# The order of wide and narrow matmuls in the products of an up projection

## The chip, the cores and the metric

The kernel runs on one core of a Trainium2 chip. The metric is device time in microseconds; a kernel's time is the median of its runs. The engines are named as in the profile: PE is the matrix engine (TensorE) and PEld its weight loads, DVE is VectorE, ACT is ScalarE, POOL is GpSimd, SP is SyncE, which issues the loads from HBM.

## The reference

One encoder layer on 512 positions with 2048 channels, all in float32. A first part (normalisation, input projection, convolution group and neighbourhood attention, output projection) ends in a residual x. The part that matters here is the gated MLP behind it:

```python
xn = rms_norm(x, ffn_norm_g[l])
up = jnp.einsum("bsd,df->bsf", xn, w_up[l])          # 2048 -> 2 x 5632
up = depthwise_conv(up, ffn_dw_w[l], ffn_dw_b[l])    # width 3 along the sequence
gate, val = jnp.split(up, 2, axis=-1)
x = x + jnp.einsum("bsf,fd->bsd", jax.nn.silu(gate) * val, w_down[l])
```

A last RMSNorm follows.

## The kernel before

Activations lie transposed: 128 channels on the partitions, 512 positions along the free axis. A float32 product is done with three products of parts: every operand is split into a high part (rounded to the matmul's format, `fp32r`) and a low part (what is left), and high x high, high x low and low x high are added up in PSUM. For weights, `parts` (L111) does the split for a tile of 8 blocks of 128 x 128: ACT writes `whi` (L114), DVE writes `wlo` (L115).

The up projection works on f = 0 to 43, each with 128 gate columns and 128 value columns. For each f the two output tiles (gate and value) by two halves of the sequence form a 2 x 2 block product, and the kernel does it with seven products instead of eight (a scheme of Strassen's kind): `factors` (L585) makes the seven combinations of weights, with DVE additions at L596 to L607, and `comb[c][k]` (tiles `xc`) holds the seven combinations of the activations, computed once. A product has eight steps k over the contraction, 8 x 128 = 1024 channels.

A tile `comb[c][k]` is 128 x 512: the high part of 256 positions in the left half, the low part in the right half. So in `up` (L638), function `product`, one matmul of 512 columns with `whi` (L648, called wide) gives high x high in the left half of a PSUM tile and high x low in the right half, and one matmul of 256 columns with `wlo` (L649, called low) adds low x high into the right half. Each matmul has its own weight load (PEld). For k = 0 the wide comes first and clears the accumulator; for k = 7 the wide comes last and closes it. In between they take turns, wide and low. Behind the last wide, `tick` (L657) lets one step of other staged work be issued and `between` (L658) may put in a stretch of the down projection. The two halves of the PSUM tile are then taken by ACT (L662, tiles `vv` and `pl`) and DVE.

The first four f go through `up_apart` (L705) instead, with three matmuls of 256 columns per step and nothing staged between. The other 40 f go through `up`: 40 x 7 = 280 products.

The down projection runs between the products, on the hidden values of the four f before: `down` (L757), two units of weights for most f, one behind product 3 and one behind product 6, each two output tiles of 4 steps with three 512-column matmuls (L125 to L127), whose result ACT copies (L768) and POOL adds into a DRAM tensor by DMA (L769).

The order of weight units is a list, `plan`, made beforehand; `weights` (L146) keeps three units ahead (`AHEAD`), with four buffers each for `whi` and `wlo` and seven for the raw tiles that SP loads. Within an engine, the program order is that of the code, apart from priorities that the first part uses.

Of the kernel before, what the change touches and what calls it, by code (L numbers as in the profile page):

```python
# [16 lines left out]
P = 128  # L17
# [17 lines left out]
U = 8  # L35
# [5 lines left out]
H = S // 2  # L41
# [25 lines left out]
def layer(ctx: ExitStack, tc: tile.TileContext, xT, w_in, w_out, w_up, w_down, par, tab, out):  # L67
    nc = tc.nc
# [16 lines left out]
    def t2(name, dt=F32):  # L85
        return tp.tile([P, S], dt, tag="t2k", name=name)
# [45 lines left out]
    def tick(behind):  # L132
        for todo in (steps, asteps):
            while todo:
                try:
                    with tc.issue_after(behind.ins):
                        next(todo[0])
                    break
                except StopIteration:
                    todo.pop(0)  # L140
# [5 lines left out]
    def weights():  # L146
        at = weights.at
        weights.at += 1
        while len(made) < min(at + 1 + AHEAD, len(plan)):
            made.append(plan[len(made)]())  # L150
        return made[at]
# [75 lines left out]
    ps = psa.tile([P, S], F32, tag="po", name="idle")  # L227
# [17 lines left out]
    for step in ORDER:  # L245
        i = next(a_ if step == "a" else q_)
# [283 lines left out]
    comb = [[] for _ in range(7)]  # L530
# [107 lines left out]
    def up(f, between):  # L638

        def product(c):  # L640

            w = weights()
            ps = (psa.tile([P, S], F32, tag="po", name="pu") if c == 6 else
                  psm.tile([P, S], F32, tag="mm", name="pu"))
            for k in range(U):
                hi, lo = (w[i][:, k * P:(k + 1) * P] for i in range(2))
                m = comb[c][k]
                wide = lambda: nc.tensor.matmul(ps, hi, m, start=k == 0, stop=k == U - 1)  # L648
                low = lambda: nc.tensor.matmul(ps[:, H:], lo, m[:, :H], start=False, stop=False)  # L649

                if k < U - 1:
                    wide()
                    i = low()
                else:
                    low()
                    i = wide()
            tick(i)  # L657
            between(c)  # L658
            return ps[:, :H], ps[:, H:]

        def copy(to, ps):
            nc.scalar.activation(to, ps, AF.Copy)  # L662

        def pair(name):
            return t2(name).rearrange("p (i t) -> p i t", i=2)

        def both(x):
            return x.unsqueeze(1).broadcast_to([P, 2, H])


        vv, low = pair("vv"), pair("pl")
        for i in range(2):
            m, l = product(i)
            copy(vv[:, i], m)
            copy(low[:, i], l)
        m7, l = product(2)
        add(vv, vv, low)
        low = pair("pl")
        copy(low[:, 0], l)
        m1, l = product(3)  # L680
        copy(low[:, 1], l)
        uu, v = pair("uu"), pair("vl")
        u, u2 = uu[:, 0], uu[:, 1]
        add(u2, m7, low[:, 0])
        add(v, vv, both(u2))
        m6, l = product(4)
        add(u, m1, low[:, 1])
        low = pair("pl")
        copy(low[:, 0], l)
        add(u2, u, m6)  # L690
        m2, l = product(5)
        add(u2, u2, low[:, 0])
        add(v, v, both(u2))
        add(vv[:, 1], vv[:, 1], u2)
        low, g = pair("pl"), pair("g")
        copy(low[:, 0], l)
        add(g[:, 0], u, m2)
        m3, l = product(6)
        copy(low[:, 1], l)
        add(g[:, 1], vv[:, 1], m3)  # L700
        add(g, g, low)
        g, v = (t.rearrange("p i t -> p (i t)") for t in (g, v))
        return g, v
# [218 lines left out]
```

## Time and profile before

| | |
|---|---|
| median of 3 runs | 2068.48 us (2067.77 to 2069.17) |
| span of the profiled execution | 2066.8 us |
| PE busy | 2046.6 us, 99% |
| DVE busy | 1664.6 us, 81% |
| ACT busy | 1065.4 us, 52% |
| granted PE clock, mean | 0.997 |
| HBM | 132 GB/s over the span |

The span runs from the first to the last instruction of one execution; the runs' times include what lies around it. Busy time of PE counts a matmul from its start to its modelled end, and matmuls overlap; so two matmuls that follow each other closely both count their whole length only where the view lists them one by one, while the busy time of the engine counts the time covered. A group's row on the page shows how many instructions it has, their busy time added up, the mean duration of one, and the idle time before them. The timeline lists single instructions by start time.

### The profile page before, as it was taken

The numbers are of one execution on the slowest core, as the hardware profiler recorded it, in microseconds if no ns is written. First come the engines' busy times: TensorE is split into PE (matmuls) and PEld (weight loads), VectorE is DVE, ScalarE is ACT, GpSimd is POOL, SyncE is SP. The second block draws the span as 40 slices with busy tenths as digits, with TensorE's granted clock in tenths as the row PEclk, the third lists the DMA queues.
The fourth block names the chain that finished last, engine by engine and source line by source line (L and its number), as shares of the span: only waits on it lengthen the run. The fifth ranks groups of instructions, "written<-read, shape, count | busy, mean of one in ns | idle before, by whom it ended". The sixth has DMA issues, their size and how long they took to land.

```text
span 2066.8 us, 28555 instructions
## 1 busy us (share of the span) xinstructions
PE 2046.6 (99%) x10810; PEld 1733.0 (84%) x10810; DVE 1664.6 (81%) x2316; ACT 1065.4 (52%) x1728; POOL 156.2 (8%) x186
## 2 busy tenths in 40 slices
PE   9999999999999999999999999999999999999997
PEld 7887888787788998888888888888888888888887
DVE  7986697687567898888888878888788888889876
ACT  6244424447445545555555555555554554555562
POOL 0000000000001001111111111111111111110110
PEclk9999999999999999999999999999999999999998
DMA  7323242335437535566566565566656566565682
GB/s 251 111 88 97 74 121 84 109 101 177 140 113 170 136 114 137 128 148 138 122 149 147 123 143 143 127 139 143 134 133 143 125 147 142 131 138 123 145 211 82
DMA packets 99113, 275.38 MB, mean 133 GB/s; under 512 B 10912, under 2 KB 15520, under 8 KB 98976
## 3 DMA queue, kind: packets, MB, share of 16 engines
q1 hardware_dynamic: 73616, 227.40, 36.3%
q0 software_dynamic: 25216, 46.15, 15.7%
q8 instruction: 85, 1.39, 0.3%
q14 instruction: 52, 0.43, 0.1%
q10 hardware_dynamic: 144, 0.01, 0.0%
HBM read 218.99 MB, written 54.53 MB: 132 GB/s over the span
## 4 chain that ended last, share of the span: by engine, by line
issue 52%; PE 39%; POOL 6%; DMA 1%; DVE 1%; ACT 1%; SPq 0%; POOLq 0%; DVEq 0%; ACTq 0%
PE pj L125 7%; PE pj L126 7%; PE pj L127 7%; POOL x2d L769 6%; PE po L125 2%; PE po L126 2%; PE po L127 2%; PE pu L648 2%; PE pd L125 1%; PE pd L127 1%; PE pd L126 1%; PE pu L649 1%; PE sc L402 1%; PE trp L432 1%; PE po L445 1%
## 5 line engine op out<-in xcount | busy, mean ns | idle before, releaser
L648 PE MATMUL pu<-xc,whi 128*128 128x512 f32 x2240 | 782.7, 398 | 0.3 <-ACT pl L662 0.3
L115 DVE TENSOR_TENSOR wlo<-raw,whi 128x1024 fp32r<-128x1024 f32 x364 | 444.2, 1221 | 252.4 <-ACT whi L114 231.1
L114 ACT ACTIVATE whi<-raw 128x1024 fp32r<-128x1024 f32 x364 | 384.3, 1058 | 471.7 <-PE pj L126 177.1
L649 PE MATMUL pu<-xc,wlo 128*128 128x256 f32 x2240 | 583.0, 281 | 0.0
L648 PEld LDWEIGHTS pu<-xc,whi 128*128 128x128 f32 x2240 | 407.9, 188 | 80.5 <-ACT pl L662 0.6
L649 PEld LDWEIGHTS pu<-xc,wlo 128*128 128x128 f32 x2240 | 422.9, 189 | 25.4
L125 PE MATMUL pj<-xh,whi 128*128 128x512 f32 x640 | 252.6, 398 | 1.6 <-DVE gate L301 1.0
L127 PE MATMUL pd<-hh,wlo 128*128 128x512 f32 x640 | 248.9, 391 | 1.4 <-DVE wlo L115 1.4
L126 PE MATMUL pj<-xl,whi 128*128 128x512 f32 x640 | 249.9, 391 | 0.1
L125 PE MATMUL pd<-hh,whi 128*128 128x512 f32 x640 | 249.9, 390 | 0.0
L127 PE MATMUL pj<-xh,wlo 128*128 128x512 f32 x640 | 249.7, 390 | 0.0
L126 PE MATMUL pd<-hl,whi 128*128 128x512 f32 x640 | 249.1, 389 | 0.0
L769 POOL DMA_DIRECT2D x2d<-pdc x160 | 139.2, 872 | 1175.0 <-ACT pdc L768 1071.9
L662 ACT ACTIVATE pl<-pu 128x256 f32<-128x256 f32 x280 | 105.0, 380 | 176.8 <-PE pu L648 176.8
L316 DVE SCALAR_TENSOR_TENSOR y<-ch,prm,y 128x508 f32<-128x508 f32 (+14 forms) x240 | 172.9, 740 | 4.1
L114 ACT ACTIVATE whi<-ws 128x1024 fp32r<-128x1024 f32 x132 | 139.7, 1058 | 68.5 <-PE pu L648 44.4
L115 DVE TENSOR_TENSOR wlo<-ws,whi 128x1024 fp32r<-128x1024 f32 x132 | 160.9, 1219 | 1.5 <-ACT whi L114 1.3
L125 PEld LDWEIGHTS pj<-xh,whi 128*128 128x128 f32 x640 | 120.2, 188 | 32.9 <-issue 3.7
L127 PEld LDWEIGHTS pd<-hh,wlo 128*128 128x128 f32 x640 | 120.2, 188 | 30.0 <-DVE wlo L115 4.9
L768 ACT ACTIVATE pdc<-pd 128x512 f32<-128x512 f32 x160 | 93.8, 588 | 95.5 <-PE pd L127 95.5
L126 PEld LDWEIGHTS pd<-hl,whi 128*128 128x128 f32 x640 | 120.2, 188 | 25.7
L126 PEld LDWEIGHTS pj<-xl,whi 128*128 128x128 f32 x640 | 120.3, 188 | 25.6 <-DVE xl L238 1.2
(172 smaller groups left out, 2774.6 us busy)
## 6 DMA issues: line engine op xcount, KB each, us to landing
raw<-in_w_up SPq DMA_DIRECT2D x176, 512.0 KB, 3.7
raw<-in_w_down SPq DMA_DIRECT2D x88, 512.0 KB, 4.0
x2d<-pdc POOLq DMA_DIRECT2D x160, 256.0 KB, 4.8
raw<-in_w_in SPq DMA_DIRECT2D x76, 512.0 KB, 4.0
raw<-in_w_out SPq DMA_DIRECT2D x32, 512.0 KB, 3.7
x<-in_xT SPq DMA_DIRECT2D x32, 256.0 KB, 5.4
tab<-in_tab SPq DMA_DIRECT2D x32, 256.0 KB, 4.6
x2d<-x SPq DMA_DIRECT2D x16, 256.0 KB, 2.0
```

The source lines that it names most:

```text
L114: i = nc.scalar.activation(hi[:, :n], raw[:, :n], AF.Copy)
L115: j = nc.vector.tensor_sub(lo[:, :n], raw[:, :n], hi[:, :n].bitcast(F32))
L125: nc.tensor.matmul(ps, hi[:, a], mh, start=start, stop=False)
L126: nc.tensor.matmul(ps, hi[:, a], ml, start=False, stop=False)
L127: return nc.tensor.matmul(ps, lo[:, a], mh, start=False, stop=stop)
L316: nc.vector.scalar_tensor_tensor(y[:, a:b], h[:, a + j - PAD:b + j - PAD], prm[:, o + j:o + j + 1], y[:, a:b], op0=ALU.mult, op1=ALU.add)
L402: m = nc.tensor.matmul(both[:, j, i, :], q[hp, b * P:(b + 1) * P], grid(k, KC0[b], KW)[hp], start=True, stop=True)
L648: wide = lambda: nc.tensor.matmul(ps, hi, m, start=k == 0, stop=k == U - 1)
L649: low = lambda: nc.tensor.matmul(ps[:, H:], lo, m[:, :H], start=False, stop=False)
L662: nc.scalar.activation(to, ps, AF.Copy)
L768: nc.scalar.activation(t, ps, AF.Copy)
L769: nc.gpsimd.dma_start(xd[d], t, accum_op=ALU.add)
```

## The change

Inside a product of `up` the sixteen matmuls are issued in another order: the wides of k = 0 to 6, then the lows of k = 0 to 7, then the wide of k = 7. Before, wide and low took turns, with the last pair swapped. The same matmuls are issued on the same operands; the first wide still clears the accumulator and the last still closes it. `up_apart` and `down` are not touched, and the order of products, down units and weight units is the same.

```diff
@@ -642,18 +642,14 @@
             w = weights()
             ps = (psa.tile([P, S], F32, tag="po", name="pu") if c == 6 else
                   psm.tile([P, S], F32, tag="mm", name="pu"))
+            def wide(k):
+                return nc.tensor.matmul(ps, w[0][:, k * P:(k + 1) * P], comb[c][k], start=k == 0, stop=k == U - 1)
+
+            for k in range(U - 1):
+                wide(k)
             for k in range(U):
-                hi, lo = (w[i][:, k * P:(k + 1) * P] for i in range(2))
-                m = comb[c][k]
-                wide = lambda: nc.tensor.matmul(ps, hi, m, start=k == 0, stop=k == U - 1)
-                low = lambda: nc.tensor.matmul(ps[:, H:], lo, m[:, :H], start=False, stop=False)
-
-                if k < U - 1:
-                    wide()
-                    i = low()
-                else:
-                    low()
-                    i = wide()
+                nc.tensor.matmul(ps[:, H:], w[1][:, k * P:(k + 1) * P], comb[c][k][:, :H], start=False, stop=False)
+            i = wide(U - 1)
             tick(i)
             between(c)
             return ps[:, :H], ps[:, H:]
```

## The prediction

> **What bounds the kernel now.** I read the page first, then the table of busy times over four stretches, then the waits of TensorE (PE), and last the timeline of PE, matmul by matmul, because the change moves nothing else.
>
> ```profile
> span 2066.8 us, 28555 instructions
> ...
> PE 2046.6 (99%) x10810; PEld 1733.0 (84%) x10810; DVE 1664.6 (81%) x2316; ACT 1065.4 (52%) x1728; POOL 156.2 (8%) x186
> ...
> L648 PE MATMUL pu<-xc,whi 128*128 128x512 f32 x2240 | 782.7, 398 | 0.3 <-ACT pl L662 0.3
> ...
> L649 PE MATMUL pu<-xc,wlo 128*128 128x256 f32 x2240 | 583.0, 281 | 0.0
> ```
>
> ```profile
> 774.00:1982.00 1208.00, 1206.32 (x6305) 1028.37 (x6305) 1007.18 (x1272) 658.24 (x1028) 132.24 (x152) 1.00 0.59 137
> ```
>
> ```profile
> PE pd L127 <- DVE wlo L115: 1.4, 8, 0.2
> ...
> PE pu L648 <- ACT pl L662: 0.3, 1, 0.3
> ```
>
> The stretch from 774 to 1982 us holds every matmul that the diff touches (columns: length, then busy time of PE, PEld, DVE, ACT, POOL, then the granted clock and DMA). PE is busy in 1206.32 of 1208.00 us at a granted clock of 1.00, DVE in 1007.18 (83%). PE's waits there are the two rows above, 1.7 us in all. So PE alone sets the end of this stretch, and what its own stream gains or loses shows in the time nearly one for one.
>
> The durations 398 and 281 ns can't be added: 782.7 + 583.0 = 1365.7 us is more than the stretch itself, in which the down matmuls must find room too. Matmuls overlap in these records. What one costs is the distance from its start to the next start, so I price by that, from the timeline (columns: start, duration, engine, line, operation; "x2" merges two of one kind).
>
> ```profile
> 1019.16 0.39 PE L648 MATMUL pu<-xc,whi 128*128 128x512 f32 x1
> 1019.38 0.28 PE L649 MATMUL pu<-xc,wlo 128*128 128x256 f32 x1
> 1019.50 0.40 PE L648 MATMUL pu<-xc,whi 128*128 128x512 f32 x1
> ...
> 1021.27 0.40 PE L648 MATMUL pu<-xc,whi 128*128 128x512 f32 x1
> 1021.50 0.40 PE L649 MATMUL pu<-xc,wlo 128*128 128x256 f32 x2
> 1021.74 0.63 PE L648 MATMUL pu<-xc,whi 128*128 128x512 f32 x2
> 1022.21 0.28 PE L649 MATMUL pu<-xc,wlo 128*128 128x256 f32 x1
> ...
> 1027.61 0.40 PE L125 MATMUL pd<-hh,whi 128*128 128x512 f32 x1
> ```
>
> From 1019.16 to 1027.61 stand exactly three products (48 matmuls): 8.45 us, 2817 ns for one, or 352 ns for a pair of one wide (512 columns) and one low (256 columns). There are 2240 / 8 = 280 products.
>
> **The change part by part.** It removes and adds no instruction. Each product issues the same eight wides and eight lows with the same sixteen weight loads; only the order inside the product differs. Order before: W L W L ... W L L W. After: seven W, eight L, one W. The price of a wide among wides and of a low among lows stands elsewhere in this trace.
>
> ```profile
> 1013.46 0.40 PE L648 MATMUL pu<-xc,whi 128*128 128x512 f32 x1
> ...
> 1015.08 0.39 PE L125 MATMUL pd<-hh,whi 128*128 128x512 f32 x1
> ...
> 1018.93 0.39 PE L127 MATMUL pd<-hh,wlo 128*128 128x512 f32 x1
> ```
>
> ```profile
> 689.65 0.39 PE L127 MATMUL po<-mbh,wlo 128*128 128x512 f32 x1
> 689.88 0.28 PE L125 MATMUL pu<-xc,whi 128*128 128x256 f32 x1
> 689.99 0.28 PE L126 MATMUL pu<-xc,whi 128*128 128x256 f32 x1
> ...
> 693.95 0.28 PE L126 MATMUL pu<-xc,whi 128*128 128x256 f32 x1
> ```
>
> - Wide among wides: 1015.08 to 1018.93 is 17 steps of the down stage: 3.85 us / 17 = 226.5 ns.
> - Low among lows: 689.99 to 693.95 is 33 steps of the first four f, whose products use 256-column matmuls only: 3.96 us / 33 = 120.0 ns. Each of them had its own weight load, and neighbours add into the same 256 columns of PSUM, as the eight lows will.
> - At these prices a product is 8 x 226.5 + 8 x 120.0 = 2772 ns. In turns it is 2817: 45 ns are lost to the turning.
>
> The grouped product still turns twice, so two transitions stay.
>
> - From wides to lows: the first 34 steps of the 256-column run (689.88 to 693.95) took 4.07 us where 34 x 120 = 4.08: about 10 ns less, a small gain, at the edge of what rows of 10 ns can tell.
> - From lows to wides: 1013.46 is the last wide of a product, behind two lows. From it to 1015.08 are seven steps of 512 columns: 1.62 us, where 7 x 226.5 = 1585 ns. So wides behind lows pay about 34 ns, spread over the first few. The same place one stretch of trace later pays less:
>
> ```profile
> 1091.96 0.40 PE L648 MATMUL pu<-xc,whi 128*128 128x512 f32 x1
> ...
> 1093.56 0.39 PE L125 MATMUL pd<-hh,whi 128*128 128x512 f32 x1
> ```
>
> Again seven steps, 1.60 us: 14 ns. I take the middle of the two, 24 ns.
>
> Net of the transitions: 24 - 10 = +14 ns. A grouped product is then 2772 + 14 = 2786 ns, 31 ns less than 2817. Over 280 products: 8.7 us. The ends: with 34 ns, the saving is 21 ns, 5.9 us; with 14 ns it is 41 ns, 11.5 us; with no transition at all 45 ns, 12.6 us.
>
> The waits that move with it:
>
> - The first low of a product waits for DVE's wlo. It was the second matmul, it becomes the eighth, some 6 x 226.5 = 1360 ns later. What is queued behind it is the other seven lows and the last wide. The row of L649 shows 0.0 us of waiting today, so nothing is won; there is only more room.
> - The last reader of whi is the last wide and the last reader of wlo the low before it, both as before. So the weight buffers, the PSUM buffer and the copies behind a product (L662) are released at the same place of the product, 31 ns earlier in time. No queue of SP, POOL, ACT or DVE is moved past: none of their instructions changes place, so the weight DMAs are issued behind the same releases.
> - The cover that must hold is DVE's slack: its 1007.18 us of work have to fit into about 1199 instead of 1208, 84% instead of 83%. If that cover were gone, DVE would have to be late in each product; it is late at 8 places only, the down matmuls waiting for wlo (1.4 us in all). There PE now comes earlier by the gain of the one to three products since the weights' buffer came free, 31 to 93 ns, and waits that much longer: 8 x 31 to 8 x 93 ns, 0.2 to 0.7 us. I take 0.4 off the gain.
>
> Sum: 8.7 - 0.4 = 8.3 us. The span goes from 2066.8 to 2058.5 us. The median of the runs, 2068.48, lies 1.7 above the profiled span, and I carry that over: 2060.2 us.
>
> **The rivals.**
>
> No change: each matmul costs what it costs in any order. Then the 45 ns belong to these operands (xc, whi and wlo in their places in memory) and not to the turning, and the product stays at 2817 ns: 2068.5 us. For it speaks that no run of more than two such wides exists in this trace. Against it: the first wide of a product behind a down matmul (1019.16, the rows above) takes 0.22 us, the same as the wides of the down stage, with the same xc and whi; it is the wides behind lows that are longer (1021.50 to 1022.21 holds two lows and two wides: 0.71 us, where 2 x 120 + 2 x 226.5 is 0.693). A page of the Trainium skill, TensorE: Matmul & The Clock Gate (section Back-to-back issue gap), has it as this rival does: a cost that follows from the columns alone, 262 cycles for 256 and 518 for 512 when warm, so an estimate from it is 8 x (109 + 216) = 2600 ns for a product in either order, and no gain. The trace does not agree with the figures (2817 ns, and 120.0 and 226.5 in pure runs).
>
> Slower: lows leave a debt that the wides pay, and the debt grows with the run of lows. Two lows left 24 ns; if that is 12 for each low, eight leave 96. The product would be 2772 + 96 - 10 = 2858 ns, 41 more than now: 280 x 41 ns = 11.5 us, 2080.0 us. It decides from 55 / 8 = 6.9 ns for each low on. Against it stands the one place where a long run of 256-column matmuls ends and wides follow:
>
> ```profile
> 773.60 0.40 PE L648 MATMUL pu<-xc,whi 128*128 128x512 f32 x1
> ...
> 776.67 0.28 PE L649 MATMUL pu<-xc,wlo 128*128 128x256 f32 x1
> ```
>
> Behind 672 of them (3 x 224, the first four f) the first product and the next wide took 3.07 us; the settled one above, 1019.16 to 1022.21, took 3.05. A debt that grew with the run would be 672 x 12 ns = 8 us here; it is some 20 ns.
>
> Larger gain: no debt at all in the new order, 12.6 us, 2055.9 us. The two places above that pay 34 and 14 ns speak against it.
>
> **How the numbers follow.** A gain between 5 and 11.5 us (the two transition prices, less the longer waits): 0.70, and the forecast is its middle, 2060.2. A larger gain: 0.05. A gain of 4.1 to 5 us, part of the loss belonging to the operands: 0.05. No change, within 0.2% (4.1 us, about what a measurement of this kernel can tell): 0.12. Slower, the growing debt: 0.08. So faster 0.80, same 0.12, slower 0.08. The range runs from 2055.5, just under the case without any debt, to 2065.5, which takes in the smallest gain and a part of the no-change case; what is left out is the rest of that case and the slower one.
>
> **What will show it.** In the timeline of the changed kernel, a product behind a down stage should last about 2.79 us from its first wide to the next matmul; the wides 2 to 7 should stand 0.226 to 0.227 us apart, where 0.232 or more means that the loss belongs to the operands; the lows should stand 0.12 us apart, where more means that a run of loads doesn't hide under 256 columns. The wide behind the eight lows and those that follow should pay 14 to 34 ns together; more than 55 makes the change a loss. PE's share should stay at 99%, its wait for wlo in the down matmuls at 1.4 to 2.1 us; above 5 us there, DVE has taken the gain back and the prediction is wrong in the cover. The mean durations of L648 and L649 say little, for the reason above.

## The result and the profile after

The changed kernel takes 2060.74 us (median of five runs, 2059.51 to 2063.47) against 2068.48 before: a ratio of 0.9962, with a 95% interval of 0.9951 to 0.9972. That is 7.7 us less; the forecast was 2060.2 us. In a second round of runs it came to 2060.78 us, ratio 0.9968 (0.9956 to 0.9981).

The page of the changed kernel has the wide on line 646 and the low on line 651:

```profile
span 2059.0 us, 28552 instructions
...
PE 2038.8 (99%) x10810; PEld 1734.1 (84%) x10810; DVE 1665.1 (81%) x2316; ACT 1065.3 (52%) x1728; POOL 156.3 (8%) x186
...
L646 PE MATMUL pu<-xc,whi 128*128 128x512 f32 x2240 | 573.5, 392 | 0.3 <-ACT pl L658 0.3
...
L651 PE MATMUL pu<-xc,wlo 128*128 128x256 f32 x2240 | 312.3, 282 | 0.0
```

The busy times of the two groups fell by 480 us (from 782.7 + 583.0 to 573.5 + 312.3) while the kernel gained 7.8 us of span, and the mean durations hardly moved (398 to 392, 281 to 282 ns). A group's busy time is not the sum of its durations (before, 2240 x 398 ns would be 891.5 us, and the row says 782.7) but the time that its matmuls cover; they overlap in these records, and matmuls of one kind that follow each other share their covered time. Neither number prices this change. The starts do. The same view of the timeline as before, three products between two pieces of the down stage (a row now covers a whole run, from the first start to the last end; two answers of the view meet at 1019.78, inside a run of wides):

```profile
1016.78 0.39 PE L127 MATMUL pd<-hh,wlo 128*128 128x512 f32 x1
1017.01 1.75 PE L646 MATMUL pu<-xc,whi 128*128 128x512 f32 x7
1018.59 1.12 PE L651 MATMUL pu<-xc,wlo 128*128 128x256 f32 x8
1019.54 0.63 PE L646 MATMUL pu<-xc,whi 128*128 128x512 f32 x2
```

```profile
1021.39 1.11 PE L651 MATMUL pu<-xc,wlo 128*128 128x256 f32 x8
1022.34 2.00 PE L646 MATMUL pu<-xc,whi 128*128 128x512 f32 x8
1024.18 1.11 PE L651 MATMUL pu<-xc,wlo 128*128 128x256 f32 x8
1025.13 0.40 PE L646 MATMUL pu<-xc,whi 128*128 128x512 f32 x1
1025.37 0.40 PE L125 MATMUL pd<-hh,whi 128*128 128x512 f32 x1
```

From 1017.01 to 1025.37 the three products take 8.36 us, 2787 ns each (8.45 and 2817 before). The seven wides behind a down stage take 1.58 us, 226 ns each. Eight lows take 0.95 us, 10 ns less than 8 x 120. Eight wides behind lows (1022.34 to 1024.18) take 1.84 us, 28 ns more than 8 x 226.5.

Over all 280 products, from the first start of each to the next matmul's start, the mean is 2819.6 ns before and 2789.6 after: 30.0 x 280 = 8.4 us. The 1824 matmuls of the down stage between them went the other way, from 418.5 to 419.7 us by their starts. Together that is 7.2 us, the gain of the whole stage (1207.97 to 1200.75 us, from the first wide to the first matmul behind the last product). The other 0.6 us of the span came ahead of the stage, whose first wide started at 772.96 us instead of 773.60; in the second profile of the changed kernel it started at 773.67, so this does not belong to the change.

The window of busy times (columns as before) and the waits of PE, after:

```profile
774.00:1974.00 1200.00, 1197.50 (x6303) 1029.47 (x6302) 1006.66 (x1271) 657.41 (x1028) 132.28 (x152) 1.00 0.60 138
...
PE pd L127 <- DVE wlo L115: 2.2, 8, 0.3
...
PE pu L646 <- ACT pl L658: 0.3, 1, 0.3
```

The wait for wlo in the down stage went from 1.4 to 2.2 us, at the same 8 places. These rows hold only the idle time behind the modelled end of the matmul before; by the starts a place costs more. One of the 8, in the changed kernel:

```profile
903.77 0.40 PE L126 MATMUL pd<-hl,whi 128*128 128x512 f32 x1
904.44 0.50 PE L127 MATMUL pd<-hh,wlo 128*128 128x512 f32 x1 [0.27 <-DVE wlo L115]
904.78 0.40 PE L125 MATMUL pd<-hh,whi 128*128 128x512 f32 x1
905.01 0.39 PE L126 MATMUL pd<-hl,whi 128*128 128x512 f32 x1
905.24 1.75 PE L646 MATMUL pu<-xc,whi 128*128 128x512 f32 x7
...
908.01 0.40 PE L127 MATMUL pd<-hh,wlo 128*128 128x512 f32 x1
```

The two steps around the wait take 1.01 us where two steps of the down stage take 0.45. Over the 8 places such steps lose 3.6 us before and 4.4 after, 0.75 us more. And PE's order there is not that of the code, in either kernel: 7 of the 24 matmuls of a down stage, then one whole product, then the other 17.

### The profile page after: what moved, and what is told of

Its sections match the earlier page's. It is cut to its first block, busy times and chain, and to the rows that moved or that the text cites. A ratio compares the mean times of both kernels' runs of the same rounds, so it can differ in the third digit from the quotient of the medians.

```text
span 2059.0 us, 28552 instructions
## 1 busy us (share of the span) xinstructions
PE 2038.8 (99%) x10810; PEld 1734.1 (84%) x10810; DVE 1665.1 (81%) x2316; ACT 1065.3 (52%) x1728; POOL 156.3 (8%) x186
## 4 chain that ended last, share of the span: by engine, by line
PE 93%; DVE 3%; DMA 1%; issue 1%; ACT 1%; SPq 0%; DVEq 0%; ACTq 0%
PE pu L646 23%; PE pu L651 12%; PE pd L127 8%; PE pd L125 8%; PE pd L126 8%; PE pj L125 7%; PE pj L126 7%; PE pj L127 7%; PE po L125 3%; PE po L126 3%; PE po L127 3%; PE pu L125 1%; PE pu L127 1%; PE pu L126 1%; DVE hl L750 1%
## 5 line engine op out<-in xcount | busy, mean ns | idle before, releaser
L646 PE MATMUL pu<-xc,whi 128*128 128x512 f32 x2240 | 573.5, 392 | 0.3 <-ACT pl L658 0.3
L651 PEld LDWEIGHTS pu<-xc,wlo 128*128 128x128 f32 x2240 | 305.6, 190 | 21.8
L651 PE MATMUL pu<-xc,wlo 128*128 128x256 f32 x2240 | 312.3, 282 | 0.0
```

The lines of the kernel that those rows point to most:

```text
L646: return nc.tensor.matmul(ps, w[0][:, k * P:(k + 1) * P], comb[c][k], start=k == 0, stop=k == U - 1)
L651: nc.tensor.matmul(ps[:, H:], w[1][:, k * P:(k + 1) * P], comb[c][k][:, :H], start=False, stop=False)
```

## The experiments

The theory: PE pays for each turn from lows (256 columns) to wides (512 columns). Behind a run of lows the next five or so wides are longer, and the first low behind wides is a little shorter, about 20 ns net where the wides are many; how long the run of lows is does not matter. The rivals: the loss belongs to the operands of this stage (the tile read twice, the columns of PSUM just written, the change from whi to wlo); it comes from lows too short to cover a weight load; or the debt grows with the number of lows.

**Blocks of four and of two.** The changed kernel with another loop inside a product (B stands for 4 or 2):

```diff
-            for k in range(U - 1):
-                wide(k)
-            for k in range(U):
-                nc.tensor.matmul(ps[:, H:], w[1][:, k * P:(k + 1) * P], comb[c][k][:, :H], start=False, stop=False)
+            for k0 in range(0, U, B):
+                for k in range(k0, min(k0 + B, U - 1)):
+                    wide(k)
+                for k in range(k0, k0 + B):
+                    nc.tensor.matmul(ps[:, H:], w[1][:, k * P:(k + 1) * P], comb[c][k][:, :H], start=False, stop=False)
             i = wide(U - 1)
```

> Order of a product WWWW LLLL WWW LLLL W: 2 turns from lows to wides. Turning theory, price of a turn between 6.4 ns (in turns, 45 ns for 7) and 17 ns (changed kernel, one): 14 ns each, product about 2772 + 28 = 2800 ns, 2063 us. Rival, the loss belongs to the operands and the changed kernel won otherwise: no regular place between the two, 2068 or 2061.

> Order of a product WW LL WW LL WW LL W LL W: 4 turns. Turning theory: about 10 ns each, product about 2812 ns, 2066.4 us. Rival as for the blocks of four.

Measured: blocks of four 2061.76 us (ratio 0.9970, 0.9958 to 0.9982), blocks of two 2066.18 us (0.9989, 0.9980 to 0.9998). The mean product is 2795.4 and 2808.1 ns. Rows of the blocks of four, a run each:

```profile
1018.41 0.64 PE L652 MATMUL pu<-xc,wlo 128*128 128x256 f32 x4
1018.88 0.86 PE L646 MATMUL pu<-xc,whi 128*128 128x512 f32 x3
1019.58 0.64 PE L652 MATMUL pu<-xc,wlo 128*128 128x256 f32 x4
```

Three wides behind lows take 0.70 us, 20 ns more than 3 x 226.5; four lows take 0.47, 10 less than 4 x 120. With the turns from lows to wides in each product, the kernels stand in one order (the column "a turn" is what the product takes over 2772 ns, divided by the turns):

| order | turns | product, ns | a turn, ns |
|---|---|---|---|
| in turns (before) | 7 | 2819.6 | 6.8 |
| blocks of two | 4 | 2808.1 | 9.0 |
| blocks of four | 2 | 2795.4 | 11.7 |
| seven, eight, one (after) | 1 | 2789.6 | 17.6 |

Fewer turns cost less in sum, and each costs more: more wides stand behind it, and the first five are the longer ones (their steps stand in the last section).

The five kernels that follow, up to the lows of 320 columns, ran once each; their product times are read from that run's trace.

**Another low beside each wide.** In turns as before, but the low behind wide k is that of k + 4:

```diff
-                hi, lo = (w[i][:, k * P:(k + 1) * P] for i in range(2))
-                m = comb[c][k]
+                hi, m = w[0][:, k * P:(k + 1) * P], comb[c][k]
+                j = (k + U // 2) % U
+                lo, ml = w[1][:, j * P:(j + 1) * P], comb[c][j]
...
-                low = lambda: nc.tensor.matmul(ps[:, H:], lo, m[:, :H], start=False, stop=False)
+                low = lambda: nc.tensor.matmul(ps[:, H:], lo, ml[:, :H], start=False, stop=False)
```

> The order in turns of the kernel before, but the low that follows the wide k is that of k + 4 (modulo 8), so that no low reads the tile of activations that the wide beside it reads. Turning theory: product 2819 ns, 2068.5 us as before. Rival, the loss in turns is the second reading of the same tile: product 2780 or less, 2057 us.

Measured: 2067.72 us, product 2819.9 ns. Reading the same tile twice in a row is not the loss.

**Lows into the left half.**

```diff
-                low = lambda: nc.tensor.matmul(ps[:, H:], lo, m[:, :H], start=False, stop=False)
+                low = lambda: nc.tensor.matmul(ps[:, :H], lo, m[:, :H], start=False, stop=False)
```

> The order in turns of the kernel before, but the lows add into the left half of the PSUM tile, not the right (the halves are summed afterwards anyway). Turning theory: product 2819 ns, 2068.5 us. Rival, the loss comes from adding into the 256 columns that the wide has just written: product 2780 ns or less, 2057 us.

Measured: 2067.93 us (the kernel before beside it: 2067.31), product 2818.9 ns. Nor is it the half of PSUM that the lows add into. A wide writes both halves, so here too the lows add into columns that a wide has just written; the lows of 512 columns, which add into all of these columns and lose nothing, answer that rival.

**Lows of 512 columns, in turns.**

```diff
-                low = lambda: nc.tensor.matmul(ps[:, H:], lo, m[:, :H], start=False, stop=False)
+                low = lambda: nc.tensor.matmul(ps, lo, m, start=False, stop=False)
```

> The order in turns of the kernel before, but each low is a matmul of all 512 columns (it adds low x low as well). Turning theory (what costs is the change of width): sixteen matmuls at 226.5 ns, product 3624 ns, 2068.5 + 280 x 0.805 = 2294 us, and flat steps of 226 to 227 ns. Rival (what costs is the change from whi to wlo or the operands of this stage): 45 ns more, 3669 ns, 2306 us.

Measured: 2288.64 us, product 3626.8 ns. The turning theory's 3624 is met, the rival's 3669 not; every step is flat:

```profile
1010.24 0.39 PE L648 MATMUL pu<-xc,whi 128*128 128x512 f32 x1
...
1012.96 0.39 PE L648 MATMUL pu<-xc,whi 128*128 128x512 f32 x1
```

Twelve steps, whi and wlo in turns, in 2.72 us: 226.7 ns. With the same tiles in the same order, taking turns costs nothing as long as the width stays. This is the run that settles that the width matters. Its time is 5 us under the expectation because the down stage lost its waits and its debts: its 1824 matmuls take 413.4 us here, 226.7 ns each, and 418.5 before.

**Lows of 320 columns, in turns and grouped.** Two kernels, with the low below in the order before and in the changed order:

```diff
-                low = lambda: nc.tensor.matmul(ps[:, H:], lo, m[:, :H], start=False, stop=False)
+                low = lambda: nc.tensor.matmul(ps[:, H - 64:], lo, m[:, :H + 64], start=False, stop=False)
```

> The order in turns of the kernel before, lows of 320 columns in place of 256 (the low part is added at the wrong place, the result is not the layer's). A pure run of 320 columns by interpolation between 120.0 and 226.5 ns: 146.6 ns, so without any loss 8 x (226.5 + 146.6) = 2985 ns. If the loss in turns is there for any change of width: 3030 ns, 2127 us. If it comes from lows that are too short to cover a weight load (the floor of 120 ns): 2985 ns, 2115 us.

> The order of the changed kernel, lows of 320 columns in place of 256 (the low part is added at the wrong place). If the loss is there for any change of width: 2985 + 17 = 3002 ns, 2119.5 us, 28 ns a product less than in turns. If it comes from lows that are too short: 2985 ns, 2115 us, the same as in turns.

Measured: 2127.66 us in turns, 2117.54 grouped; products 3027.5 and 3003.0 ns. The grouped kernel's rows:

```profile
1001.68 1.33 PE L651 MATMUL pu<-xc,wlo 128*128 128x320 f32 x8
1002.85 2.00 PE L646 MATMUL pu<-xc,whi 128*128 128x512 f32 x8
1004.69 1.33 PE L651 MATMUL pu<-xc,wlo 128*128 128x320 f32 x8
```

Eight lows take 1.17 us, 146 ns each, as interpolated; the eight wides behind them 1.84 us, the same 28 ns too much as behind lows of 256. The time of the grouped kernel lies between its two forecasts, 2119.5 and 2115 us; the product decides, 3003.0 ns where the theory has 3002 and the rival 2985. Lows a quarter wider leave the same debt, so it is not a floor of 120 ns under lows of 256 columns. The pure steps also lie on one line: 26.7 ns for the 64 columns from 256 to 320, 80.0 for the 192 from 320 to 512.

One form of that rival stays untested. A weight load lasts longer than the step of either low, by the profile of the changed kernel (mean 190 ns):

```profile
L651 PEld LDWEIGHTS pu<-xc,wlo 128*128 128x128 f32 x2240 | 305.6, 190 | 21.8
```

No run has lows whose step is longer than a load and still shorter than a wide's, so the runs do not tell whether such lows would leave a debt too.

**Products in pairs.** The changed kernel, with products 0 and 1, 2 and 3, 4 and 5 issued two by two. Both weight units are taken at once; the pair 2 and 3 writes a PSUM tile of the attention stage, which is idle by then:

```diff
+        def products(*cs):
+            ws = weight_pair() if len(cs) == 2 else (weights(),)
...
+            for i in n:
+                for k in range(U - 1):
+                    wide(i, k)
+            for i in n:
+                for k in range(U):
+                    nc.tensor.matmul(pss[i][:, H:], ws[i][1][:, k * P:(k + 1) * P], comb[cs[i]][k][:, :H], start=False, stop=False)
+            for i in n:
+                m = wide(i, U - 1)
+                tick(m)
+            between(cs[-1])
```

> Products 0 and 1, 2 and 3, 4 and 5 are issued two by two: fourteen wides, sixteen lows, two wides; product 6 as in the changed kernel. 4 turns from lows to wides for each f in place of 7. Turning theory (a turn costs about 20 ns net behind a long run of lows, however long the run): 3 turns fewer x 20 ns x 40 f = 2.4 us less than the changed kernel, about 2058.3 us, if the weights (now released two by two) still come in time. Rival, a debt that grows with the number of lows: no gain, 2060.7. Rival, weights late: PE waits for wlo or whi in products, more than 3 us, and the time is over 2061.

> The same kernel as the pairs, beside the triple on one chip: 2056.0 us if the first runs hold. Its first profile had a wait of 2.3 us in the first product of the first four f; if that belongs to the order it is there again, if it is chance it is not.

> The changed kernel beside the two others on one chip: 2060.7 us if the first runs hold, 4.8 us over the pairs. By turns alone it would be 2.4 us; the rest is the wait for wlo in the down stage, at 8 places, which the pairs' profile does not have.

Measured: 2055.97 us (ratio 0.9937, 0.9923 to 0.9950) and in the second round 2053.94 us (0.9934, 0.9922 to 0.9947), beside 2060.78 of the changed kernel. This beats both kernels, and by more than the turns explain.

```profile
1023.14 3.82 PE L652 MATMUL pu<-xc,whi 128*128 128x512 f32 x16
1026.79 2.08 PE L661 MATMUL pu<-xc,wlo 128*128 128x256 f32 x16
1028.70 0.63 PE L652 MATMUL pu<-xc,whi 128*128 128x512 f32 x2
1029.17 0.39 PE L125 MATMUL pd<-hh,whi 128*128 128x512 f32 x1
```

Sixteen wides behind sixteen lows take 3.65 us, 26 ns more than 16 x 226.5: the debt did not grow with the run of lows. The mean product is 2780.4 ns, 9.3 less than the changed kernel's 2789.7 in the same round: 2.6 us, where 2.4 was expected. The other part is the down stage: its matmuls take 414.7 us in place of 419.6. Most of that, 4.4 us, are the long steps at the 8 places: in the pairs every down stage stands whole, 24 matmuls in a row, and the waits for wlo are gone from the list (second round):

```profile
775.00:1968.00 1193.00, 1193.00 (x6306) 1030.89 (x6305) 999.75 (x1271) 645.73 (x1027) 132.53 (x152) 1.00 0.59 138
```

```profile
PE pu L125 <- ACT xc L535: 1.5, 1, 1.5
```

PE now covers every microsecond of the stretch (first the window of busy times, as before; then the one wait of PE around the up stage, in its first product). That wait was 0.6 us before and is 2.3 and 1.5 us in the two profiles of the pairs, 0.8 us in the second one of the changed kernel; the stage starts 1.4 us later than there, so some of the gain is given back. Why the pairs keep the down stage whole and DVE in time for it was not tried.

**A triple.** The pairs, with 4, 5 and 6 issued together:

```diff
-        (m6, l), (m2, l2) = products(4, 5)
+        (m6, l), (m2, l2), (m3, l3) = products(4, 5, 6)
```

> As the pairs, but products 4, 5 and 6 are issued together: 3 turns from lows to wides for each f in place of 4. Turning theory: 20 ns x 40 f = 0.8 us less than the pairs, about 2055.2 us. Rival, weights released three at once come late: PE waits for whi or wlo behind the triple in most f, 10 us or more over the pairs.

Measured: 2072.85 us, ratio 1.0025 (1.0016 to 1.0034), a miss for the theory's forecast. The rival's time came, 10 us or more over the pairs, but not its wait for weights. The trace shows two things:

```profile
1049.95 1.75 PE L651 MATMUL pu<-xc,whi 128*128 128x512 f32 x7
1051.53 1.11 PE L660 MATMUL pu<-xc,wlo 128*128 128x256 f32 x8
1052.49 2.08 PE L651 MATMUL pu<-xc,whi 128*128 128x512 f32 x8
1054.41 1.10 PE L660 MATMUL pu<-xc,wlo 128*128 128x256 f32 x8
1055.35 3.59 PE L651 MATMUL pu<-xc,whi 128*128 128x512 f32 x15
1058.77 2.08 PE L660 MATMUL pu<-xc,wlo 128*128 128x256 f32 x16
```

```profile
774.00:1986.00 1212.00, 1199.83 (x6299) 1029.06 (x6298) 979.16 (x1263) 634.69 (x1023) 132.73 (x152) 1.00 0.56 136
```

```profile
PE pd L125 <- ACT hh L761: 9.7, 8, 2.7
```

PE's order is not the order of the code: the pair 0 and 1 stands apart, so most f have four turns again, as with the pairs (4.65 for each f over all 40), and nothing is won. And PE is idle for 12.2 of the 1212 us, 9.7 of them for the hidden values that ACT splits ahead of the down stage and 2.5 in one product, for ACT's copy `pl`. So this run shows what this attempt at a group of three costs this pipeline, and says nothing of the price of a turn.

## Why the prediction was right

- PE sets the end of the stage, and its stream is priced by starts: held. PE is busy in 1197.50 of 1200 us after, 1206.32 of 1208 before, and the stage's 7.2 us are 8.4 won in the products less 1.2 lost in the down stage.
- A wide among wides at 226.5 and a low among lows at 120.0 ns, taken from other stages, hold in this one: 1.58 us / 7 and, behind the first two lows, 120 ns. So the 45 ns were the turning and not the operands; the runs with 512 columns, with another low beside the wide and with the left half show it.
- The saving for each product, 31 ns forecast, is 30.0. Inside that sum the price of the turn to wides was taken as the mean of two places, 24 ns; in the changed order it is 28 at every place (26 and 28 by the rows of pairs and of 320 columns). The lower of the two places was special to the order in turns: by the starts, the seven steps that were read there take about 1.602 us at 30 places of the trace before and 1.614 at 47 (the other 8 hold a wait), and after the change 1.614 or 1.615 at all 77 that hold no wait. The first lows gain 8 ns, 10 forecast. That the saving fits to 1 ns is partly luck: the product was put some 3 ns too low both in turns (2817 for 2819.6) and grouped (2786 for 2789.6), and the difference hides it.
- The wait for wlo in the down stage: 0.4 us taken off, 0.2 to 0.7 given, 0.8 measured (1.4 to 2.2), a little over the end of the bound. By the starts the down stage lost 1.2 us; the part that is not waiting is the debt of the lows, now always the larger one, paid by the down matmuls behind products 3 and 6. The forecast had priced that debt inside the products, and so one sign that it gave is off: a product behind a down stage lasts 2.77 us (1017.01 to 1019.78), not 2.79.
- No change by operands, at 0.12, and the growing debt, at 0.08: neither is borne out. Sixteen lows leave the same debt as eight and as the 672 before the first product of this stage. The Trainium skill's page TensorE: Matmul & The Clock Gate (section Back-to-back issue gap) gives, for a matmul taken by itself, a gap that follows from the columns alone; the traces agree inside runs of one width, with other figures (226.7 and 120 ns), and not where widths take turns (2819.6 against 2789.6 ns for the same columns).

What the debt is inside the engine stays open. The runs show where it arises (behind lows of 256 or 320 columns), who pays (the next wides) and how much; none shows the mechanism.

## What to carry to other kernels

Where PE is the bound, price matmuls from start to start, in pure runs and in the mix that the kernel has; the difference is what the order costs, and the profile before holds both numbers if any stage runs one width alone. Group matmuls of one width as far as PSUM and weight buffers allow: each change from narrow to wide costs some 20 ns net here where five or more wides follow, behind 8 lows as behind 16. Larger groups need their inputs earlier and free their buffers later; two products at once fitted this pipeline and gained more than the turns, the attempt at three lost it all. Read a wait from the starts too: here the idle time that the profile listed was half of what the places cost, or less (2.2 of 4.4 us, 1.4 of 3.6).

## What was not expected of the hardware

The debt has a fixed shape. From the starts in the trace of the changed kernel, the wides behind a run of lows step by 234, 236, 228, 232 and 231 ns and then by 227, and the first lows behind wides by 113, 119 and then 120, in nearly every product, and in the down matmuls behind a product just the same. In turns this became a cycle of three pairs, 233, 117, 241, 120, 236, 113 ns, 353 ns a pair instead of 346.5. A wide that follows a single low already pays.
